# The first layer's rope: both halves copied crosswise by ScalarE, one product with sin on VectorE

## The chip, the core and the metric

The kernel runs on one core of a Trainium2 chip. TensorE (PE in the profile) multiplies matrices into PSUM, VectorE (DVE) and ScalarE (ACT) read PSUM and SBUF and write them, GpSimd (POOL) does small work and some DMAs, and SyncE (SP) issues most DMAs. Each engine works through a queue of its own in order and waits at semaphores for the others. The metric is the device time of one execution in microseconds.

## The reference, cut to what matters

A decoder trunk of two layers on a sequence of 512 positions with a width of 1024, in fp32. The first ("even") layer has 8 heads of retention and, beside them, 8 blocks of a gated linear recurrence (RG-LRU). The second ("odd") layer is differential attention. Both turn q and k by rotary embedding (rope):

```python
def rope(x, pos):
    half = x.shape[-1] // 2
    ...
    x1 = x[..., :half].astype(jnp.float32)
    x2 = x[..., half:].astype(jnp.float32)
    return jnp.concatenate([x1 * cos - x2 * sin, x2 * cos + x1 * sin], axis=-1)

def retention(q, k, v):
    ...
    scores = jnp.einsum('bnihd,bnjhd->bnhij', qc, kc) * decay
    ...

def even_layer(...):
    proj = jnp.einsum('bsd,de->bse', x, w_in)
    q, k, v, g_ret, xb, g_lru = jnp.split(proj, [...], axis=-1)
    q = rope(q.reshape(B, S, RET_HEADS, RET_DK), pos)
    k = rope(k.reshape(B, S, RET_HEADS, RET_DK), pos) * (RET_DK ** -0.5)
    ret = retention(q, k, v.reshape(B, S, RET_HEADS, RET_DV))
```

## The kernel before

**Products.** Every fp32 operand of a product is split into a high and a low half (`split`, L146: a cast to `..h`, by ScalarE as a rule, then on VectorE the difference `..l`, L153), and each product is three matmuls: high by high, low by high, high by low (`mm3`, L155 to L157). Weights come by DMA as raw tiles `w_r` and are split in the same way, so ScalarE and VectorE also carry the weights w0, w1 and on: 1024 columns each.

**The first layer.** Activations lie transposed: a unit (`t_unit`, L196) multiplies one weight tile by x and leaves a tile of 128 channels by 512 positions in one PSUM bank. A list `ev` (L273) sets the order of the units: for heads 0 to 5 in turn the gates gl and gr, the input xb of the recurrence, q and k; v and the output products (out, lo, ro, eo) between them; heads 6 and 7 have another order. The bank pool of the units, `ps_pj`, has four banks, so a unit waits until the tile of four units ago is out of its bank. The scores have two banks (`ps_sc`).

- q and k (L595 to L599): the unit's bank goes through `rope` (L347), which leaves the halves q0h, q0l and so on. L356 multiplies the bank by cos into the tile c; L360 and L361 multiply its lower and upper 64 partitions by sin crosswise into the tile s; L362 adds; `split` follows.
- Retention (`retention`, L479), per head: scores rs from k and q in four blocks (512, 384, 256 and 128 columns), their product with the decay (L487, rsd), the product ro with v, the norm (L498 to L516: squares, a sum by matmul, Ln, Exp, Square, products), then the gate gr (L520) and a split into retm.
- The recurrence (`lru`, L523), per block: ScalarE takes xb from its bank (L526, L528), VectorE adds three taps (L531), xc is split, two products with gate weights (pr, pi), Sigmoid, Tanh, Ln, Exp and Sqrt on ScalarE (L540 to L556, with loads of function tables between them), products on VectorE, a scan (L560), the gate gl (L563).
- Output products: each has its banks summed into y by VectorE (L262, L264).

**Order.** TensorE's and SyncE's queues are written in program order. `Side` (L54) places the matmuls of retention and recurrence between those of the units: a job runs its next piece a set number of ticks later, a tick being one step of three matmuls. VectorE's and ScalarE's queues are put in order by the framework's scheduler, with priorities such as `P_ROPE`.

**The second layer** uses the same `rope` with `swap=True` (L878): ScalarE copies the two halves of the bank crosswise into s (L353, L354), and VectorE multiplies s by sin in one operation (L358) and subtracts (L362). The table `sin` holds the negative in its lower partitions (L950), which is why one form adds and the other subtracts.

Of the kernel before, what the change touches and what calls it, by code (L numbers as in the profile page):

```python
# [11 lines left out]
ALU = mybir.AluOpType  # L12
# [91 lines left out]
def trunk(ctx: ExitStack, tc: tile.TileContext, a):  # L104
    nc = tc.nc
# [22 lines left out]
    def work(name):  # L128
        return wk.tile([P, S], F32, tag="wk", name=name)
# [4 lines left out]
    def bank(pl, tag, name):  # L134
        return pl.tile([P, 512], F32, tag=tag, name=name)

    def pair(pl, shape, tag, name, **kw):
        return tuple(pl.tile(shape, F32R, tag=tag + x, name=name + x, **kw) for x in "hl")
# [4 lines left out]
    def cut(t, *ix):  # L143
        return t[0][ix], t[1][ix]

    def split(src, dst, scale=None, copy=nc.scalar.copy):  # L146
        if scale is not None:
            s = sg[:, scale:scale + 1]
            nc.scalar.activation(out=dst[0], in_=src, func=AF.Identity, scale=s)
            nc.vector.scalar_tensor_tensor(out=dst[1], in0=src, scalar=s, in1=dst[0].bitcast(F32), op0=ALU.mult, op1=ALU.subtract)  # L150
            return
        copy(out=dst[0], in_=src)  # L152
        return nc.vector.tensor_tensor(out=dst[1], in0=src, in1=dst[0].bitcast(F32), op=ALU.subtract)  # L153

    def mm3(out, l, r, start, stop, kinds=range(3), **kw):  # L155
        for n in kinds:
            nc.tensor.matmul(out=out, lhsT=l[n == 2], rhs=r[n == 1], start=start and n == 0, stop=stop and n == 2, **kw)  # L157

    def load(name, shape, src, pl=None, tag=None, bufs=None):
        t = (pl or const).tile(shape, F32, tag=tag or name, name=name, bufs=bufs)  # L160
        nc.sync.dma_start(out=t, in_=src)
        return t
# [27 lines left out]
    def take(ahead):  # L190
        taken[0] += 1
        while len(ready) < min(taken[0] + ahead, len(order)):
            list(fetch())
        return ready[taken[0] - 1]

    def t_unit(act, name):  # L196
        w = take(2)
        ps = bank(ps_pj, "pj", name + "_ps")
        for kt in range(KT):
            mm3(ps, cut(w, ALL, slice(kt * P, kt * P + P)), cut(act, ALL, kt), kt == 0, kt == KT - 1)  # L200
            side.tick()
        return ps
# [78 lines left out]
    for kind, i in ev:  # L281
        if kind in ("ro", "lo", "out"):
            order += [(eo[2 * i + j + n], None) for n in {"ro": (0,), "lo": (8,), "out": (8, 0)}[kind] for j in range(2)]
        else:
            n = 4 if kind == "v" else 1
# [58 lines left out]
    nhalf = const.tile([P, SB], F32, tag="nhalf", name="nhalf")  # L344
    nc.gpsimd.memset(nhalf, -0.5)

    def rope(ps, tag, name, swap=False):  # L347
        with tc.high_priority(P_ROPE):
            s = work(name + "_s")
            h = P // 2  # L350
            if swap:

                nc.scalar.copy(out=s[:h], in_=ps[h:])  # L353
                nc.scalar.copy(out=s[h:], in_=ps[:h])  # L354
            c = work(name + "_c")
            nc.vector.tensor_tensor(out=c, in0=ps, in1=cos, op=ALU.mult)  # L356
            if swap:
                nc.vector.tensor_tensor(out=s, in0=s, in1=sin, op=ALU.mult)  # L358
            else:
                nc.vector.tensor_tensor(out=s[:h], in0=ps[h:], in1=sin[h:], op=ALU.mult)  # L360
                nc.vector.tensor_tensor(out=s[h:], in0=ps[:h], in1=sin[:h], op=ALU.mult)  # L361
            nc.vector.tensor_tensor(out=c, in0=c, in1=s, op=ALU.subtract if swap else ALU.add)  # L362
            r = pair(qkp, [P, S], tag, name)
            split(c, r)
        return r
# [64 lines left out]
    sin = load("sin", [P, S], a["sin"])  # L430
# [152 lines left out]
    for kind, i in ev:  # L583
        if kind == "v":
            if i:
                for j in range(4):
                    side.need(job["ret", j], lambda: j in seen)
            v = v_even(i)
        elif kind == "xb":
            if i % 2 == 0:  # L590
                raw = load(f"gw{i}", [P, 4 * P], a["gw"][i // 2], pl=es, tag="es")
                gw[0] = pair(two, [P, 4 * P], "gw", f"gw{i}", bufs=1)
                split(raw, gw[0])
            job["lru", i] = side.add(lru(i, t_unit(x, f"xb{i}"), mixes(("lru", i // 2))), "lru", 2)
        elif kind == "q":  # L595
            dec[i] = load(f"dec{i}", [P, S], a["dec"][i], pl=two, tag="dec")
            q[i] = rope(t_unit(x, f"q{i}"), "q", f"q{i}")
        elif kind == "k":
            job["ret", i] = side.add(retention(i, q.pop(i), rope(t_unit(x, f"k{i}"), "k", f"k{i}"), v, dec.pop(i), mixes(("ret", i // 2))), "ret", 1, RET_START[i])  # L599
        elif kind in ("ro", "lo", "out"):  # L600
            even_out({"ro": ("ret",), "lo": ("lru",), "out": ("lru", "ret")}[kind], i, f"{kind}{i}")
        else:
            ps = t_unit(x, f"{kind}{i}")
            if len(users) >= 5:
                side.need(job[users[-5]])
            users.append(("ret" if kind == "gr" else "lru", i))
            g = gp.tile([P, S], F32, tag="g", name=f"{kind}{i}")
            silu(ps, g, f"{kind}{i}")
            gates[kind, i] = g
        if (kind, i) == ("gr", 1):  # L610
            for sb in range(SB):
                nc.sync.dma_start(out=y[:, sb], in_=a["x"][sb])
# [4 lines left out]
    h = pair(big, [P, KT, S], "x", "h")  # L617
# [257 lines left out]

    def qk_unit(n, name):
        nonlocal units
        r = rope(t_unit(h, name), n, name, True)  # L878
        if units in later:
            later.pop(units)()  # L880
        units += 1
        return r
# [4 lines left out]
    for kind, i in od:  # L887
# [17 lines left out]
        elif kind == "g":  # L905
            def evac(sb, ps):
                past(i - 1)
                if sb % 2 == 0:
                    pairs[sb] = gp.tile([P, 2, S], F32, tag="g", name=f"og{i}{sb}")
                gates[sb, i] = pairs[sb - sb % 2][:, sb % 2]  # L910
                silu2(ps, gates[sb, i], work(f"og{i}{sb}_t"))

            pairs = {}
            s_unit(h, f"og{i}", False, evac)
            side.need(summed)
            scratch.close()
            qkp = pool("qkp2", 4)
            es = pool("es2", 2)
            mask = load("mask", [P, S], a["mask"], pl=es, bufs=1)
            swap()  # L920
        elif kind == "gv":
            gates_values(i)
        elif kind == "qk":
            om[i] = mix_pair(f"om{i}") if i < 7 else None
            qk = [[qk_unit(n, f"{n}{i}{mp}o") for mp in range(2)] for n in "qk"]
            om[i] = om[i] or cut(pair(big, [P, KT, S], "x", "om7"), ALL, slice(0, 2))
            for qb in range(SB):
                oj[i, qb] = side.add(attention(i, qb, *qk, om[i]), "att", 3, ATT_START[i], ATT_GAP[i])
        else:
            odd_out(i, f"oo{i[0]}", apart=True)  # L930
            if i[0] < 4:
                swap()
# [85 lines left out]
```

## Time and profile before

| what | value |
|---|---|
| median of 3 runs | 919.75 us (919.56 to 919.87) |
| the profiled execution's own time | 920.12 us |
| its span, first to last instruction | 918.4 us |
| granted TensorE clock | 0.997 |
| VectorE, 100 to 150 us: busy | 44.51 of 50 us |
| ScalarE, 50 to 100 us: busy | 37.03 of 50 us |
| DMA from HBM and to it, over the span | 193 GB/s |

The first layer takes about the first 450 us of the span. A row of a timeline has its start, its duration, engine, line, operation, output and inputs, shape, and in brackets the idle time before it with what ended it. Tiles are shown without their buffer numbers, so rq is one name for the squares of all heads; weights keep theirs (w20l). The first matmuls of heads 0, 1, 2 and 7 with their k stand at 66.68, 99.83, 133.24 and 354.03 us.

### The profile page before, as it was taken

To read this page: it belongs to the slowest core of one execution; us is meant where nothing else is said; L and a number is where in the kernel's file an instruction comes from. 1 tells how busy PE (TensorE), PEld (TensorE's weight loads), DVE (VectorE), ACT (ScalarE), POOL (GpSimd) and SP (SyncE) were. 2 spreads that over 40 slices of the span, in tenths; PEclk is the share of its full clock that TensorE was granted. 3 is DMA by queue.
4 is the path that set the end of the run, shared out by engine and by line. 5 is a ranking of instruction groups with operands and counts; after the bars stand their busy time and mean duration, and the time that the engine had idled before them with its cause. 6 is when DMAs were issued, how large, how long until landed. Compare 5 with 4: busy or idle time off the path is not lost.

```text
span 918.4 us, 11868 instructions
## 1 busy us (share of the span) xinstructions
PE 904.9 (99%) x4256; PEld 749.9 (82%) x4256; DVE 717.7 (78%) x1191; ACT 516.3 (56%) x843; POOL 111.6 (12%) x190
## 2 busy tenths in 40 slices
PE   8999999999999999999999999999999999999996
PEld 6888887888888888888888878888888888888885
DVE  5877977958868998897868887748877668877687
ACT  5567787647565668533456666435655355665440
POOL 2310010110102010010101120000120100201112
PEclk9999999999999999999999999999999999999998
DMA  8995463772829371434851226647237382187102
GB/s 279 279 290 149 121 189 92 241 207 58 262 67 287 107 191 64 167 131 149 317 187 70 69 70 228 227 164 252 70 134 248 146 319 93 58 286 249 50 1 91
DMA packets 46522, 152.92 MB, mean 167 GB/s; under 512 B 6144, under 2 KB 6272, under 8 KB 45696
## 3 DMA queue, kind: packets, MB, share of 16 engines
q1 hardware_dynamic: 41472, 135.39, 41.4%
q0 software_dynamic: 4992, 16.78, 9.3%
q8 instruction: 33, 0.54, 0.2%
q14 instruction: 25, 0.20, 0.1%
HBM read 139.57 MB, written 37.75 MB: 193 GB/s over the span
## 4 chain that ended last, share of the span: by engine, by line
PE 85%; DVE 7%; ACT 3%; issue 2%; POOL 1%; DMA 1%; SPq 0%; DVEq 0%; ACTq 0%; POOLq 0%
PE oo_ps L157 7%; PE gr_ps L157 5%; PE out_ps L157 4%; PE q_ps L157 4%; PE gl_ps L157 4%; PE ev_ps L157 4%; PE k_ps L157 4%; PE xb_ps L157 4%; PE po L157 3%; PE as L157 3%; PE ov_ps L157 2%; PE gv3a L157 2%; PE gv2a L157 2%; PE eo_ps L157 2%; PE og_ps L157 2%
## 5 line engine op out<-in xcount | busy, mean ns | idle before, releaser
L670 ACT ACTIVATE e<-as,nm 128x128 f32<-128x128 f32 (+3 forms) x64 | 33.2, 523 | 34.1 <-DVE nm L667 33.9
L677 POOL TENSOR_SCALAR zr<-z 128x1 f32<-128x1 f32 x32 | 16.3, 510 | 248.2 <-ACT e L670 248.2
L709 DVE SCALAR_TENSOR_TENSOR o<-po,ars,og 128x256 f32<-128x256 f32 x32 | 15.5, 484 | 36.8 <-POOL ars L374 36.8
L185 POOL DMA_DIRECT2D t<-t x24 | 18.9, 788 | 158.5 <-DMA t<-in_od_w 152.3
L185 POOL DMA_DIRECT2D t<-in_od_w x24 | 19.0, 793 | 118.6 <-DMA t<-in_od_w 118.6
L706 POOL TENSOR_SCALAR ave<-ss,zr 128x1 f32<-128x1 f32 x32 | 15.8, 493 | 141.7 <-ACT po L703 133.5
L667 DVE CUSTOM_DVE_ANT_0 as<-as,mask 128x128 f32<-128x128 f32 (+3 forms) x64 | 30.5, 507 | 2.3 <-PE as L157 2.3
L703 ACT ACTIVATE po<-po 128x256 f32<-128x256 f32 x32 | 11.9, 371 | 25.5 <-PE po L157 25.3
L548 DVE TENSOR_TENSOR xbp<-xbp,xc 128x512 f32<-128x512 f32 x8 | 5.5, 691 | 17.5 <-ACT xbp L545 17.5
L374 POOL TENSOR_TENSOR ars<-ave,nhalf 128x1 f32<-128x1 f32 x32 | 18.7, 586 | 2.7
L678 DVE SCALAR_TENSOR_TENSOR e<-e,zr,e 128x128 f32<-128x128 f32 (+3 forms) x32 | 17.6, 549 | 0.8
L531 DVE SCALAR_TENSOR_TENSOR xc<-xbp,vecs,xc 128x509 f32<-128x509 f32 (+2 forms) x24 | 17.9, 745 | 0.2
L264 DVE TENSOR_TENSOR y<-oo_ps,y 128x512 f32<-128x512 f32 x24 | 16.0, 684 | 2.2 <-PE oo_ps L157 2.2
L374 POOL TENSOR_TENSOR lrs<-lve,nhalf 128x1 f32<-128x1 f32 x8 | 7.4, 919 | 84.6 <-DVE lve L387 84.6
L487 DVE TENSOR_TENSOR rsd<-rs,dec 128x512 f32<-128x512 f32 (+3 forms) x32 | 15.5, 486 | 2.1 <-PE rs L157 2.1
L540 ACT ACTIVATE t<-pr,vecs 128x512 f32<-128x512 f32 x8 | 5.5, 688 | 17.5 <-PE pr L157 17.5
L682 PE MATMUL wt<-ident,e 128*128 128x128 f32 x80 | 13.9, 272 | 0.0
L152 ACT CAST hh<-ht 128x512 fp32r<-128x512 f32 x8 | 4.7, 587 | 15.7 <-PE ht L627 15.7
L682 PEld LDWEIGHTS wt<-ident,e 128*128 128x128 f32 x80 | 10.5, 140 | 3.4
L556 ACT ACT_TABLE_LOAD x8 | 10.3, 1283 | 4.2 <-DVE xc L555 4.1
L670 ACT ACTIVATION_READ_ACCUMULATOR e<-as,nm 128x1 f32 x64 | 12.5, 195 | 0.0
L675 DVE RECIPROCAL zr<-z 128x1 f32<-128x1 f32 x32 | 5.2, 162 | 9.2 <-ACT e L670 9.1
(2833 smaller groups left out, 3473.2 us busy)
## 6 DMA issues: line engine op xcount, KB each, us to landing
w_r<-in_od_w SPq DMA_DIRECT2D x58, 512.0 KB, 5.8
w_r<-in_ev_w SPq DMA_DIRECT2D x47, 512.0 KB, 4.9
t<-in_od_w SPq DMA_DIRECT2D x48, 256.0 KB, 5.4
sx<-sd SPq DMA_DIRECT2D x24, 512.0 KB, 6.1
w_r<-t SPq DMA_DIRECT2D x24, 512.0 KB, 3.2
w_r<-in_ev_wo SPq DMA_DIRECT2D x16, 512.0 KB, 4.7
w_r<-in_od_wo SPq DMA_DIRECT2D x16, 512.0 KB, 4.6
t<-in_od_w POOLq DMA_DIRECT2D x24, 256.0 KB, 5.5
```

The source lines that it names most:

```text
L157: nc.tensor.matmul(out=out, lhsT=l[n == 2], rhs=r[n == 1], start=start and n == 0, stop=stop and n == 2, **kw)
L185: nc.gpsimd.dma_start(out=dst, in_=two, max_dma_last_dim=4 * D, accum_op=ALU.add)
L264: nc.vector.tensor_tensor(out=yy, in0=ps, in1=yy, op=ALU.add)
L374: nc.gpsimd.tensor_tensor(out=out, in0=var, in1=nhalf[:, :1], op=ALU.pow)
L487: nc.vector.tensor_tensor(out=s[:, :n], in0=ps[:, :n], in1=dec[:, :n], op=ALU.mult)
L531: nc.vector.scalar_tensor_tensor(out=xc[:, sh:], in0=xb[:, :S - sh], scalar=conv_w(w, c), in1=xc[:, sh:], op0=ALU.mult, op1=ALU.add)
L667: nc.vector.tensor_tensor_reduce(out=ps[:, :n], in0=ps[:, :n], in1=mask[:, S - n:], scale=-QK_SCALE, scalar=3.0e38, op0=ALU.add, op1=ALU.m ...
L670: nc.scalar.activation(out=e, in_=ps[:, :n], func=AF.Exp, scale=-1.0, bias=nm, accum_out=z[:, mp:mp + 1])
L677: nc.gpsimd.tensor_scalar(out=zr[:, 1:2], in0=z[:, 0:1], scalar1=z[:, 0:1], scalar2=EPS, op0=ALU.mult, op1=ALU.mult)
L678: nc.vector.scalar_tensor_tensor(out=ee[0], in0=ee[1], scalar=zr[:, 0:1], in1=ee[0], op0=ALU.mult, op1=ALU.add)
L682: nc.tensor.transpose(out=pt[:, kb * P:kb * P + P], in_=ee[0][:, kb * P:kb * P + P], identity=ident)
L706: nc.gpsimd.tensor_scalar(out=ve, in0=ss, scalar1=zr[:, 1:2], scalar2=None, op0=ALU.add)
```

## The change

`rope` loses its argument `swap`: every call now takes the form with two ScalarE copies of 64 partitions, one product with sin over 128 partitions, and a subtraction. It concerns the 16 ropes of the first layer (8 heads, q and k). The 16 of the second layer stay as they are.

```diff
-    def rope(ps, tag, name, swap=False):
+    def rope(ps, tag, name):
         with tc.high_priority(P_ROPE):
             s = work(name + "_s")
             h = P // 2
-            if swap:
-                nc.scalar.copy(out=s[:h], in_=ps[h:])
-                nc.scalar.copy(out=s[h:], in_=ps[:h])
+            nc.scalar.copy(out=s[:h], in_=ps[h:])
+            nc.scalar.copy(out=s[h:], in_=ps[:h])
             c = work(name + "_c")
             nc.vector.tensor_tensor(out=c, in0=ps, in1=cos, op=ALU.mult)
-            if swap:
-                nc.vector.tensor_tensor(out=s, in0=s, in1=sin, op=ALU.mult)
-            else:
-                nc.vector.tensor_tensor(out=s[:h], in0=ps[h:], in1=sin[h:], op=ALU.mult)
-                nc.vector.tensor_tensor(out=s[h:], in0=ps[:h], in1=sin[:h], op=ALU.mult)
-            nc.vector.tensor_tensor(out=c, in0=c, in1=s, op=ALU.subtract if swap else ALU.add)
+            nc.vector.tensor_tensor(out=s, in0=s, in1=sin, op=ALU.mult)
+            nc.vector.tensor_tensor(out=c, in0=c, in1=s, op=ALU.subtract)
...
-        r = rope(t_unit(h, name), n, name, True)
+        r = rope(t_unit(h, name), n, name)
```

The order of instructions on TensorE, GpSimd and SyncE is the same before and after. On ScalarE 32 copies join and on VectorE 16 products go, and the scheduler puts these two queues in another order in the first layer. The lines behind `rope` have numbers lower by 5 in the changed kernel.

ScalarE's queue in head 1, from the Ln of the recurrence's block 1 (r1) on, before (ro0 and rq0 are head 0's retention and its squares):

```order
L552 ACTIVATE r1_847<-t1_835 128x512
L553 ACT_TABLE_LOAD
L553 ACTIVATE r1_847<-r1_847 128x512
L498 ACTIVATE rq0_876<-ro0_863 128x512
L152 CAST rq0h_878<-rq0_876 128x512
L152 CAST q1h_888<-q1_c_883 128x512
L556 ACT_TABLE_LOAD
L556 ACTIVATE r1_847<-t1_835 128x512
L509 ACT_TABLE_LOAD
L509 ACTIVATE rq0_876<-rv0_925,epsb_119 128x512
```

The same piece of ScalarE's queue now:

```order
L547 ACTIVATE r1_849<-t1_837 128x512
L352 COPY q1_s_884<-q1_ps_804 64x512
L493 ACTIVATE rq0_878<-ro0_865 128x512
L353 COPY q1_s_884<-q1_ps_804 64x512
L152 CAST rq0h_880<-rq0_878 128x512
L548 ACT_TABLE_LOAD
L548 ACTIVATE r1_849<-r1_849 128x512
L152 CAST q1h_891<-q1_c_887 128x512
L551 ACT_TABLE_LOAD
L551 ACTIVATE r1_849<-t1_837 128x512
L352 COPY k1_s_942<-k1_ps_903 64x512
L353 COPY k1_s_942<-k1_ps_903 64x512
```

The Exp of r1 (L553, now L548) has moved behind q1's copies, the square and the cast of rq0, and k1's two copies stand between the Sqrt (L556, now L551) and the norm's Ln.

VectorE's queue ahead of xc2l, the low half of the recurrence's block 2, for which TensorE's pr2 waits, before:

```order
L153 TENSOR_TENSOR w19l_1107<-w19_r_1105,w19h_1106 128x1024
L531 SCALAR_TENSOR_TENSOR xc2_1062<-xbp2_1060,vecs_203,xc2_1062 128x509
L153 TENSOR_TENSOR r11l_1054<-rsd11_1051,r11h_1053 128x384
L531 SCALAR_TENSOR_TENSOR xc2_1062<-xbp2_1060,vecs_203,xc2_1062 128x510
L487 TENSOR_TENSOR rsd12_1084<-rs12_1080,dec1_792 128x256
L531 SCALAR_TENSOR_TENSOR xc2_1062<-xbp2_1060,vecs_203,xc2_1062 128x511
L457 TENSOR_TENSOR gr2_1099<-gr2_ps_1043,gr2_sg_1100 128x512
L487 TENSOR_TENSOR rsd13_1121<-rs13_1117,dec1_792 128x128
L153 TENSOR_TENSOR r12l_1087<-rsd12_1084,r12h_1086 128x256
L153 TENSOR_TENSOR w20l_1185<-w20_r_1183,w20h_1184 128x1024
L153 TENSOR_TENSOR r13l_1124<-rsd13_1121,r13h_1123 128x128
L153 TENSOR_TENSOR xc2l_1068<-xc2_1062,xc2h_1067 128x512
```

The same piece now:

```order
L526 SCALAR_TENSOR_TENSOR xc2_1066<-xbp2_1064,vecs_203,xc2_1066 128x509
L153 TENSOR_TENSOR w19l_1111<-w19_r_1109,w19h_1110 128x1024
L526 SCALAR_TENSOR_TENSOR xc2_1066<-xbp2_1064,vecs_203,xc2_1066 128x510
L482 TENSOR_TENSOR rsd13_1125<-rs13_1121,dec1_794 128x128
L526 SCALAR_TENSOR_TENSOR xc2_1066<-xbp2_1064,vecs_203,xc2_1066 128x511
L153 TENSOR_TENSOR r13l_1128<-rsd13_1125,r13h_1127 128x128
L153 TENSOR_TENSOR r12l_1091<-rsd12_1088,r12h_1090 128x256
L452 TENSOR_TENSOR gr2_1103<-gr2_ps_1047,gr2_sg_1104 128x512
L153 TENSOR_TENSOR w20l_1190<-w20_r_1188,w20h_1189 128x1024
L153 TENSOR_TENSOR xc2l_1072<-xc2_1066,xc2h_1071 128x512
```

rsd13 has moved ahead of the last tap of xc2 (128x511), and r13l and r12l ahead of gr2; w20l stands just ahead of xc2l in both.

VectorE's queue in head 6, from k6's rope to the sums of the product lo into y, before:

```order
L362 TENSOR_TENSOR k6_c_2821<-k6_c_2821,k6_s_2820 128x512
L153 TENSOR_TENSOR r53l_2852<-rsd53_2849,r53h_2851 128x128
L554 SCALAR_TENSOR_TENSOR xc6_2694<-t6_2773,r6_2785 128x512
L153 TENSOR_TENSOR k6l_2827<-k6_c_2821,k6h_2826 128x512
L555 SCALAR_TENSOR_TENSOR xc6_2694<-xc6_2694,r6_2785 128x512
L153 TENSOR_TENSOR r52l_2808<-rsd52_2805,r52h_2807 128x256
L264 TENSOR_TENSOR y_202<-lo2_ps00_2840,y_202 128x512
L264 TENSOR_TENSOR y_202<-lo2_ps01_2841,y_202 128x512
L264 TENSOR_TENSOR y_202<-lo2_ps10_2866,y_202 128x512
```

The same piece now, from the product with cos on:

```order
L355 TENSOR_TENSOR k6_c_2836<-k6_ps_2765,cos_212 128x512
L153 TENSOR_TENSOR r53l_2866<-rsd53_2863,r53h_2865 128x128
L356 TENSOR_TENSOR k6_s_2833<-k6_s_2833,sin_214 128x512
L264 TENSOR_TENSOR y_202<-lo2_ps00_2854,y_202 128x512
L357 TENSOR_TENSOR k6_c_2836<-k6_c_2836,k6_s_2833 128x512
L552 SCALAR_TENSOR_TENSOR t6_2786<-t6_2786,xc6_2706 128x512
L553 SCALAR_TENSOR_TENSOR r6_2798<-r6_2798,xc6_2706 128x512
L153 TENSOR_TENSOR k6l_2841<-k6_c_2836,k6h_2840 128x512
L554 TENSOR_TENSOR r6_2798<-r6_2798,xbp6_2704 128x512
L264 TENSOR_TENSOR y_202<-lo2_ps01_2855,y_202 128x512
L555 SCALAR_TENSOR_TENSOR xc6_2706<-t6_2786,r6_2798 128x512
L264 TENSOR_TENSOR y_202<-lo2_ps10_2880,y_202 128x512
```

The two gate operations on xc6 (L554 and L555, now L549 and L550) and r52l have moved ahead of k6's rope, and the three sums into y, which stood together, now stand one by one between the rope's and the recurrence's operations.

## The prediction

> **What bounds the kernel now.** I read the page's busy line first, then who waited for whom with TensorE as the waiting engine, then TensorE's timeline at those waits.
>
> ```profile
> PE 904.9 (99%) x4256; PEld 749.9 (82%) x4256; DVE 717.7 (78%) x1191; ACT 516.3 (56%) x843; POOL 111.6 (12%) x190
> ```
> TensorE has no room: only work that holds it up can move the end. The wait view up to 450 us, which holds the first layer, names four such waits after the start-up:
>
> ```profile
> PE out_ps L157 <- ACT xc L528: 0.5, 1, 0.5
> PE pr L157 <- DVE xc7l L153: 0.4, 1, 0.4
> PE out_ps L157 <- DVE gl L457: 0.3, 1, 0.3
> PE rs L157 <- DVE rsd L487: 0.2, 1, 0.2
> ```
> A matmul row (0.39 us) outlasts the 0.23 us between two starts, so the true delay is read from the starts:
>
> ```profile
> 114.17 0.39 PE L157 MATMUL pr<-xc2h,gw2h 128*128 128x512 f32 x1
> 114.53 0.50 PE L157 MATMUL pr<-xc2l,gw2h 128*128 128x512 f32 x1
> ...
> 139.08 0.40 PE L157 MATMUL out_ps<-w22h,lrum0l 128*128 128x512 f32 x1
> 139.83 0.50 PE L157 MATMUL out_ps<-w21h,lrum0h 128*128 128x512 f32 x1 [0.35 <-DVE gl L457]
> ...
> 140.40 0.40 PE L157 MATMUL out_ps<-w21h,lrum0l 128*128 128x512 f32 x1
> 141.03 0.38 PE L157 MATMUL rs<-q2h,k2h 128*128 128x256 f32 x1 [0.24 <-DVE rsd L487]
> ...
> 141.95 0.40 PE L157 MATMUL out_ps<-w22h,lrum0l 128*128 128x512 f32 x1
> 142.84 0.51 PE L157 MATMUL out_ps<-w21h,lrum0h 128*128 128x512 f32 x1 [0.50 <-ACT xc L528]
> ...
> 342.61 0.39 PE L157 MATMUL pr<-xc7h,gw6h 128*128 128x512 f32 x1
> 343.39 0.50 PE L157 MATMUL pr<-xc7l,gw6h 128*128 128x512 f32 x1 [0.40 <-DVE xc7l L153]
> ```
> Less 0.23 for each pair, and with the 0.1 by which the second matmul after a wait comes late: 0.25 at pr2, 1.9 between 139 and 143, 0.67 at pr7, some 0.2 at pr3 near 149, read the same way. **About 3.0 us is all that a faster first layer can win**; everything else there is TensorE at full pitch. All four waits are for VectorE and ScalarE, so these two stretches count:
>
> ```profile
> 83.00:100.00 17.00, 17.00 (x80) 14.22 (x79) 14.49 (x22) 15.18 (x19) 0.78 (x1) 1.00 0.12 17
> ...
> 100.00:115.00 15.00, 15.00 (x69) 12.18 (x69) 15.00 (x25) 10.04 (x16) 1.56 (x2) 1.00 0.65 188
> 116.00:143.00 27.00, 25.91 (x117) 20.68 (x116) 21.89 (x33) 23.77 (x30) 3.93 (x5) 1.00 0.56 156
> ```
> (columns: TensorE, weight loads, VectorE, ScalarE). ScalarE is the fuller of the two in 83-100 (15.18 of 17) and in 116-143 (23.77 of 27); between them VectorE has no pause at all (15.00 of 15).
>
> **What an edit costs.** Removed and added per rope:
>
> ```profile
> L360 DVE TENSOR_TENSOR q_s<-q_ps,sin x8: 693/693/693, 53.3 to 338.2; 64x512 f32<-64x512 f32 x8
> L361 DVE TENSOR_TENSOR q_s<-q_ps,sin x8: 683/684/685, 54.0 to 338.9; 64x512 f32<-64x512 f32 x8
> ...
> L358 DVE TENSOR_TENSOR q00o_s<-q00o_s,sin x1: 681/681/681, 462.1 to 462.1; 128x512 f32<-128x512 f32 x1
> L353 ACT COPY q00o_s<-q00o_ps x1: 585/585/585, 460.3 to 460.3; 64x512 f32<-64x512 f32 x1
> ```
> A half costs VectorE as much as a whole tile, so a rope saves 0.69 there, 11 us in 16 ropes, and ScalarE gets two copies of 0.585, 19 us in all. Matmuls and DMAs keep their order; only ScalarE's and VectorE's orders change. Neither total is on the path; what is new there is a wait, shown by the second layer, which already does it so:
>
> ```profile
> 460.29 0.58 ACT L353 COPY q00o_s<-q00o_ps 64x512 f32<-64x512 f32 x1
> 460.88 0.58 ACT L354 COPY q00o_s<-q00o_ps 64x512 f32<-64x512 f32 x1
> ...
> 461.50 0.69 DVE L356 TENSOR_TENSOR q00o_c<-q00o_ps,cos 128x512 f32<-128x512 f32 x1
> ```
> The product with cos, which reads the same PSUM bank, starts only after the second copy ends (461.46). So VectorE's queue now stands still whenever ScalarE comes late to the copies. Before, L356 needed TensorE alone.
>
> **Step 1, head 1 (83 to 116).** The chain is walked through the new rows of the order, each with its duration and spacing from these rows of before.
>
> ```profile
> 86.56 0.63 ACT L553 ACTIVATE r<-r 128x512 f32<-128x512 f32 x1
> 90.49 0.63 ACT L556 ACTIVATE r<-t 128x512 f32<-128x512 f32 x1
> 95.15 0.63 ACT L511 ACTIVATE rq<-rsd 128x512 f32<-128x512 f32 x1
> ...
> 98.80 0.69 DVE L153 TENSOR_TENSOR k1l<-k_c,k1h 128x512 fp32r<-128x512 f32 x1
> 110.66 0.74 DVE L531 SCALAR_TENSOR_TENSOR xc<-xbp,vecs,xc 128x511 f32<-128x511 f32 x1
> 113.79 0.69 DVE L153 TENSOR_TENSOR xc2l<-xc,xc2h 128x512 fp32r<-128x512 f32 x1
> ...
> 99.83 0.40 PE L157 MATMUL rs<-q1h,k1h 128*128 128x512 f32 x1
> 106.59 0.28 PE L157 MATMUL rs<-q1h,k1h 128*128 128x256 f32 x1
> ```
> The Exp of r (86.56) gets q1's copies, the square and rq0h ahead of it: 88.82. VectorE's gate update waits for it, rope's difference stands behind that, q1h behind the difference; so the Sqrt (90.49) starts at 92.72. k1's copies stand behind it: the square of rsd (95.15) starts at 98.41. k1h and the rest of k1l follow: k1l starts at 99.66 (0.86 late) and ends at 100.35, just when its matmul (third of the scores at 99.83) wants it. From there VectorE's saturated stretch begins late and holds more: lrum0l (0.6) and rsd13 (0.2), which stood outside it, and 0.5 of waits for lrum0h. The last tap of xc2 (110.66) starts at 112.86. On the way the first product with dec of head 1 ends at 107.28 where the matmul at 106.59 wants its bank: TensorE loses 0.7. Then r13l, r12l, gr2 and w20l stand ahead of xc2l as before: 115.81 to 116.50, so pr2's second matmul starts at 116.52, not 114.53: **+2.0 us**, the 0.7 included. Nothing hides it, since the xc2l of before was already 0.25 late. Lower bound +0.6 (only k1l's lateness arrives, less the 0.25), upper +2.6.
>
> **Step 2, head 2 and out0 (116 to 149).** ScalarE is nearly full here, and four copies (2.3) join while w23's cast (1.06) moves behind; the Sqrt stands earlier. Set from pr2's end, the evacuation of xb3 (L526, L528), for which TensorE waits at 142.84, stands behind retm0h, which waits for L520; walked through, it ends as long after pr2 as before, within 0.1. With pr2 2.2 later on ScalarE it ends at 145.0: TensorE resumes 2.2 late. k2l, now behind the scan, makes the scores wait 1.1 at 135, and the waits at 139.08 and 140.40 go, but both lie under the last one. xc3l then needs no wait at 149 (-0.2). After step 2 the sum stands at **+2.0**. Bounds +0 (those 2 us of waits swallow step 1) and +3.
>
> **Heads 0 and 3 to 5: 0.** The same walk ends k0l at 67.03 where its matmul starts at 67.15; in heads 3 to 5 k's low half is ready over 2 us early. Without that cover a rope's chain is 0.4 longer each time (two copies 1.17, less one 0.69).
>
> **Step 3, heads 6 and 7 (300 to 357).**
>
> ```profile
> 315.11 0.39 PE L157 MATMUL lo_ps<-w49h,lrum2h 128*128 128x512 f32 x1
> 319.75 0.39 PE L157 MATMUL lo_ps<-w49h,lrum2h 128*128 128x512 f32 x1
> 321.11 0.39 PE L157 MATMUL lo_ps<-w49h,lrum2h 128*128 128x512 f32 x1
> ...
> 316.13 1.88 DVE L264 TENSOR_TENSOR y<-lo_ps,y 128x512 f32<-128x512 f32 x3
> ...
> 354.50 0.40 PE L157 MATMUL rs<-q7h,k7l 128*128 128x512 f32 x1
> 351.22 0.60 ACT L152 CAST k7h<-k_c 128x512 fp32r<-128x512 f32 x1
> ```
> k6's copies run behind the Exp of r6 (to 314.3); the product with cos gives k6's bank back at 315.46, where lo wants it at 315.11: +0.4. The three sums into y no longer stand together (316.13) but between rope and gate rows: the second ends at 320.65, the third at 322.4. lo21 (319.75, now 320.14) and lo30 (321.11) wait for them: +1.3 together. At 343 the wait for xc7l goes, since it now stands ahead of rope's difference and without two products: -0.67. But k7's copies, w58h and two activations stand ahead of k7h: 353.6 instead of 351.22, and k7l ends at 354.95, each 1.3 later with the shift. Its matmul (354.50) starts at 356.26: **+1.8** for step 3. Bounds -0.7 (only the xc7l wait goes) and +2.5.
>
> **Sum.** +2.0 and +1.8: 3.8 us. The profiled execution took 920.12 us (span 918.4, 1.7 around it); the runs' median, 919.75, is 0.4 lower, so 919.75 + 3.8 = 923.5 us.
>
> **Rivals.** *VectorE's saving decides (faster).* VectorE is full in 100-115, and all four waits lead through it; with 0.69 less per rope it could come early. If k1l is ready before 100.3 and xc2l before 114.2, all 3.0 us go: 916.7 us. Against it: the rope is fed by ScalarE, which in 83-100 has 1.8 us of pause for 2.3 us of copies. The deciding point is that k1l. [...]
>
> *Swallowed (no change).* TensorE's old waits at 139-143 take up step 1, and step 3 ends near the -0.67 and +1.3 of its first half: +0 to +1.8, some 921 us. For it: the ends of step 1 hang on a few tenths at 100.35 and 107.28. Against: the evacuation of xb3 follows pr2.
>
> *More of it (slower still).* Ropes hold the bank and the work tiles longer; if each of the remaining heads too loses 0.4 us, 2 us come on top: 925.5.
>
> **Chances.** Forecast 0.59, swallowed 0.24, faster 0.12, more 0.05. 0.2% is 1.8 us, about what a measurement of this kernel can tell from no change: slower by more 0.64, within 0.25, faster by more 0.11. The range is the sum of the bounds of steps 2 (which holds step 1) and 3 on 919.75: 0 and -0.7 give 919.0, 3 and 2.5 give 925.3; it leaves out the faster case and the one of more, 0.17.
>
> **What would show it.** Right: L356's idle time names L353/L354's copies in heads 0 to 7; k1l ends near 100.4; pr2's second matmul starts near 116.5; out_ps resumes near 145; lo's matmuls wait for L264; head 7's scores wait for k7. Wrong: pr2 at 114 to 115 (step 1 falls), TensorE resuming before 143 (the faster rival), or no wait between 315 and 322 (step 3).

## The result, and the profile after

| | before | after |
|---|---|---|
| median | 920.15 us (919.56 to 920.66, 6 runs) | 926.81 us (925.84 to 927.38, 6 runs) |
| ratio | | 1.0072 [1.0062, 1.0082] |
| span of the profiled execution | 918.4 us | 925.2 us |

The change makes the kernel 6.7 us slower. The page of the changed kernel, busy times of the engines:

```profile
PE 907.7 (98%) x4256; PEld 749.7 (81%) x4256; DVE 707.1 (76%) x1175; ACT 535.5 (58%) x875; POOL 112.1 (12%) x190
```

VectorE is 10.6 us shorter and ScalarE 19.2 longer, as counted. TensorE does the same matmuls and waits more. Who waits for whom with TensorE as the waiting engine, 20 to 450 us, changed kernel (total, times, longest):

```profile
PE pr L157 <- DVE xc2l L153: 1.1, 1, 1.1
PE rs L157 <- ACT k7h L152: 1.0, 1, 1.0
PE out_ps L157 <- ACT xc L523: 0.7, 1, 0.7
PE rs L157 <- DVE k2l L153: 0.7, 1, 0.7
PE pi L157 <- DVE rsd L482: 0.6, 1, 0.6
PE rs L157 <- ACT k2h L152: 0.5, 1, 0.5
PE rs L157 <- DVE rsd L482: 0.4, 1, 0.4
PE rs L157 <- DVE k0l L153: 0.2, 1, 0.2
PE lo_ps L157 <- DVE y L264: 0.2, 1, 0.2
```

Two of the four old waits are gone (for the gate gl, and xc7l); k's halves, which nobody waited for, now make up four lines. A wait hides the end of the matmul ahead of it (a row lasts 0.39 us, two starts stand 0.23 apart), so I compared the starts of the same matmul in both traces. TensorE's timeline of the changed kernel, at the places where its distance to before grows:

```profile
67.92 0.50 PE L157 MATMUL rs<-q0h,k0l 128*128 128x512 f32 x1 [0.20 <-DVE k0l L153]
...
100.86 0.50 PE L157 MATMUL rs<-q1h,k1h 128*128 128x512 f32 x1
...
101.67 0.50 PE L157 MATMUL rs<-q1h,k1l 128*128 128x512 f32 x1
...
108.60 0.38 PE L157 MATMUL rs<-q1h,k1h 128*128 128x256 f32 x1 [0.39 <-DVE rsd L482]
...
117.79 0.50 PE L157 MATMUL pr<-xc2l,gw2h 128*128 128x512 f32 x1 [1.11 <-DVE xc2l L153]
...
137.19 0.50 PE L157 MATMUL rs<-q2h,k2h 128*128 128x512 f32 x1 [0.51 <-ACT k2h L152]
...
138.64 0.50 PE L157 MATMUL rs<-q2h,k2l 128*128 128x512 f32 x1 [0.71 <-DVE k2l L153]
...
146.97 0.50 PE L157 MATMUL out_ps<-w21h,lrum0h 128*128 128x512 f32 x1 [0.72 <-ACT xc L523]
...
310.86 0.50 PE L157 MATMUL pi<-xc6h,gw6h 128*128 128x512 f32 x1 [0.60 <-DVE rsd L482]
...
360.20 0.50 PE L157 MATMUL rs<-q7h,k7h 128*128 128x512 f32 x1 [1.03 <-ACT k7h L152]
...
360.93 0.50 PE L157 MATMUL rs<-q7h,k7l 128*128 128x512 f32 x1
```

Added lateness by stretch, each the start here less the start before, less what was late already:

| stretch | forecast | measured |
|---|---|---|
| start-up to 12 us (not the change) | none | +0.38 |
| head 0, third matmul of the scores | 0 | +0.39 |
| head 1, up to pr2's second matmul | +2.0 | +2.48 (0.25, 0.35, 0.63, 1.25) |
| head 2 and out0, net after 153 us | 0 | +0.71 |
| heads 3 to 5 | 0 | within 0.1 |
| heads 6 and 7 | +1.8 | +2.47 (pi6 0.78, lo 0.77, pr7 -0.42, scores of head 7 1.34) |
| second layer | none | +0.3 |

A wait also makes the next matmul 0.1 late (behind k2h's wait the starts are 137.19 and 137.53, 0.34 apart instead of 0.23); in this table and below, that 0.1 stands with the next place. With its own 0.1, head 0 costs 0.47, head 1 2.38, and heads 6 and 7 cost 2.55 (pi6 0.87, lo 0.80, pr7 -0.66, scores of head 7 1.54). The start-up differs by -0.6 to +0.5 us between the traces of all runs, which are alike up to there, and the second layer by up to 1.6 (head1), so neither row is the change's.

The windows of the changed kernel (TensorE, weight loads, VectorE, ScalarE) show who got emptier:

```profile
83.00:100.00 17.00, 17.00 (x79) 14.19 (x79) 10.63 (x16) 15.32 (x20) 0.78 (x1) 1.00 0.19 44
100.00:115.00 15.00, 14.53 (x65) 11.19 (x64) 14.32 (x24) 12.01 (x19) 0.78 (x1) 1.00 0.39 118
116.00:143.00 27.00, 24.67 (x110) 19.59 (x110) 19.49 (x28) 24.14 (x32) 3.16 (x4) 1.00 0.59 161
```

In 83-100 VectorE falls from 14.49 to 10.63 us: far more than two ropes save, so work has moved out of this stretch. The timelines of ScalarE and VectorE there show why:

```profile
85.50 0.63 ACT L547 ACTIVATE r<-t 128x512 f32<-128x512 f32 x1
86.15 0.58 ACT L352 COPY q_s<-q_ps 64x512 f32<-64x512 f32 x1
86.76 0.60 ACT L493 ACTIVATE rq<-ro 128x512 f32<-128x512 f32 x1
87.38 0.58 ACT L353 COPY q_s<-q_ps 64x512 f32<-64x512 f32 x1
...
89.92 0.63 ACT L548 ACTIVATE r<-r 128x512 f32<-128x512 f32 x1
91.91 0.62 ACT L152 CAST q1h<-q_c 128x512 fp32r<-128x512 f32 x1 [1.36 <-DVE q_c L357]
```
```profile
87.99 0.69 DVE L355 TENSOR_TENSOR q_c<-q_ps,cos 128x512 f32<-128x512 f32 x1 [3.08 <-ACT q_s L353]
88.64 0.69 DVE L153 TENSOR_TENSOR rq0l<-rq,rq0h 128x512 fp32r<-128x512 f32 x1
89.25 0.69 DVE L356 TENSOR_TENSOR q_s<-q_s,sin 128x512 f32<-128x512 f32 x1
```

VectorE stands 3.08 us for ScalarE's second copy, which stands behind an Ln and a square; then ScalarE stands 1.36 us for VectorE's difference. The two in-order queues hold each other up in turn. VectorE's waits for a second copy, 20 to 450 us:

```profile
DVE q_c L355 <- ACT q_s L353: 8.6, 3, 3.1
DVE k_c L355 <- ACT k_s L353: 3.1, 1, 3.1
```

So VectorE stands still for a copy in four of the sixteen ropes only (q0, q1, q4 and k7), and q4's wait costs TensorE nothing. In the other twelve, other work fills VectorE's queue until the copies are done. In all 48 ropes of this trace the product with cos begins behind the end of the second copy out of the same bank, by 0.03 to 1.08 us (at q1 the copy ends at 87.96 and the product starts at 87.99).

### The profile page after: what moved, and what is told of

The parts are those of the page before. It is cut to its first block, busy times and chain, and to the rows that moved or that the text cites. A ratio compares the mean times of both kernels' runs of the same rounds, so it can differ in the third digit from the quotient of the medians.

```text
span 925.2 us, 11892 instructions
## 1 busy us (share of the span) xinstructions
PE 907.7 (98%) x4256; PEld 749.7 (81%) x4256; DVE 707.1 (76%) x1175; ACT 535.5 (58%) x875; POOL 112.1 (12%) x190
## 4 chain that ended last, share of the span: by engine, by line
PE 76%; ACT 9%; DVE 9%; issue 3%; DMA 2%; POOL 1%; SPq 0%; DVEq 0%; ACTq 0%; POOLq 0%
PE oo_ps L157 6%; PE out_ps L157 4%; PE ev_ps L157 4%; PE q_ps L157 4%; PE gr_ps L157 4%; PE xb_ps L157 3%; PE gl_ps L157 3%; PE po L157 3%; PE as L157 2%; PE ov_ps L157 2%; PE gv3a L157 2%; PE eo_ps L157 2%; PE og_ps L157 2%; PE k_ps L157 2%; PE gv3b L157 2%
## 5 line engine op out<-in xcount | busy, mean ns | idle before, releaser
L549 DVE SCALAR_TENSOR_TENSOR xc<-t,r 128x512 f32<-128x512 f32 x8 | 5.5, 692 | 11.0 <-ACT r L548 11.0
L677 PEld LDWEIGHTS wt<-ident,e 128*128 128x128 f32 x80 | 10.5, 140 | 3.4
L708 PEld LDWEIGHTS po<-ident,o 128*128 128x128 f32 x64 | 8.9, 140 | 4.2
```

Of the source, the lines that this page charges most:

```text
L677: nc.tensor.transpose(out=pt[:, kb * P:kb * P + P], in_=ee[0][:, kb * P:kb * P + P], identity=ident)
```

## The experiments

Theory A, from the first reading: TensorE is late where k or xc has no cover, because a link of rope now runs through ScalarE. Rivals: B, ScalarE's added time costs the same wherever it stands; C, the loss is an accident of the scheduler's new order. D came later: what counts is what stands behind the copies in ScalarE's queue.

All medians are of 4 to 11 executions, against the kernel before in the same series (919.98 to 920.26).

| run | median us | against before | ratio, 95% interval |
|---|---|---|---|
| heads012 | 924.26 | +4.1 | [1.0033, 1.0058] |
| heads345 | 920.31 | +0.2 | [0.9993, 1.0010] |
| heads67 | 922.84 | +2.7 | [1.0018, 1.0041] |
| head1 | 922.88 | +2.9 | [1.0019, 1.0042] |
| heads02 | 921.61 | +1.4 | [1.0007, 1.0025] |
| konly | 922.79 | +2.7 | [1.0017, 1.0039] |
| qonly | 923.23 | +3.1 | [1.0019, 1.0044] |
| occupancy | 928.84 | +8.7 | [1.0079, 1.0110] |
| occupancy_behind | 927.92 | +7.8 | [1.0068, 1.0096] |
| vector_saving | 920.16 | +0.2 | [0.9994, 1.0012] |
| cos_first | 923.52 | +3.4 | [1.0024, 1.0049] |
| before_vector_cast | 918.73 | -1.25 | [0.9979, 0.9996] |
| change_vector_cast | 929.25 | +9.3 | [1.0082, 1.0110] |
| cos_first_vector_cast | 925.41 | +5.15 | [1.0050, 1.0077] |
| before_low_priority | 921.90 | +1.7 | [1.0008, 1.0026] |
| change_low_priority | 929.41 | +9.2 | [1.0087, 1.0114] |

### Which heads

The kernel before, with the copies only where a name is listed (here for heads 6 and 7; the others alike):

```diff
-            s = work(name + "_s")
+            s, swap = work(name + "_s"), swap or name in ("q6", "k6", "q7", "k7")
```

heads012: 

> Copies only in heads 0 to 2 (6 of 16 ropes); heads 3 to 7 as before. Theory A (the loss is made where k or the convolution's low half is only just in time, so that TensorE waits for a chain that now runs through the copies): +3.6 us over the kernel before, with TensorE late by about 0.4 at 67, 0.6 at 100, 0.6 at 107, 1.2 at 115 and 4 at 150 us, and nothing after that. Theory B (ScalarE's added work costs the same wherever it stands): 6 of 16 parts of the 6.7 us, +2.5 us, spread evenly. Theory C (a new order in the two queues shifts waits at random): no prediction by head; the sites of the full change would not come back.

heads345: 

> Copies only in heads 3 to 5. Theory A: k's low half is 1.4 to 3.7 us early there even in the changed kernel, so 0 (within 0.3 us). Theory B: +2.5 us. Theory C: anything between -1 and +2.5.

heads67: 

> Copies only in heads 6 and 7. Theory A: the stretch from 300 to 357 us as in the full change: +0.8 where pi6's bank waits for rsd51, +0.8 at lo's two matmuls, -0.4 at pr7, +1.3 at head 7's scores: +2.5 us in all. Theory B: 4 of 16 parts, +1.7 us. Theory C: not these sites.

Measured +4.1, +0.2 and +2.7: together 7.0, where the whole change is 6.7. TensorE's sites are those of the full change to 0.1 us (in heads67: pi6 +0.75, lo +0.77, pr7 -0.42, head 7's scores +1.33). Theory A holds by place, B falls: six ropes of heads 3 to 5 cost nothing that can be measured. C in its plain form falls too, since the sites come back one by one.

head1: 

> Copies only in head 1 (q1 and k1). In the run with heads 0 to 2, TensorE lost 0.4 by 70 us, 2.5 at 100 to 115 us, and 0.9 net from 133 to 150 us. If step 1 of the prediction holds (q1's copies push the Exp, k1's stand behind the Sqrt, k1l and the convolution's xc2l come late): xc2l's matmul late by 2.0 to 2.5 us here too, about as much as there without head 0's 0.4. If step 2 holds (the shift persists through the old waits at 139 to 143, since the evacuation of the recurrence's input follows): +2.0 to +2.5 us over the kernel before at the end. If the old waits swallow it: +0.3 to +1. If head 0's lateness was needed for it: xc2l late by less than 1.

TensorE's timeline of head1, pr2's second matmul:

```profile
116.62 0.50 PE L157 MATMUL pr<-xc2l,gw2h 128*128 128x512 f32 x1 [1.09 <-DVE xc2l L153]
```

It stands 2.1 us behind its place before, 2.4 if one counts from the 0.30 by which this execution was ahead at 12 us. After 143 us it is 2.8 by the same count, 0.4 of it from lrum0's gate at 139.83: the old waits there swallow nothing. So step 1 and its persistence hold with head 0 untouched.

heads02: 

> Copies only in heads 0 and 2. Head 1 alone gave 2.5 us by the sites up to 150 us, heads 0 to 2 together 3.7. If each head has its own price: +1.2 us (k0l 0.4 late at 67, k2l late at 133). If the waits at 139 to 143 us swallow head 2's own lateness unless head 1 has used them up: head 0's 0.4 alone arrives, +0 to +0.6, and k2l's wait shows at 133 to 135 but is given back by 143.

k2's scores are late by 1.24 and 0.98 at 133 us. The profiled execution also shows TensorE at half its clock for 3.4 us here (0.51 from 137.30 to 140.75, last section), which adds 1.6; 2.1 of the whole is given back between 139 and 150. The median, +1.4, in which most executions lack the half clock, less head 0's 0.47 leaves some 0.9 for head 2, not far from the 0.71 of the full change. So the old waits swallow a part of head 2's lateness, without head 1 as with it, and the number for swallowing it whole (+0 to +0.6) was wrong. With head1's +2.9 the +1.4 adds up to the 4.1 of heads012 within the intervals.

konly and qonly, the same edit by q and k:

konly: 

> Copies only in the 8 ropes of k. Theory A1 (k's own chain to its low half is longer, and the scores wait for it): nearly the whole loss, +4 to +6 us, at 67, 100, 133 and 354 us. Theory A2 (the walk of the prediction: q1's copies push the Exp of the recurrence back, and everything of head 1 behind it): about half, +2.5 to +4 us; k1's low half is late by about 0.6 instead of 0.9 and xc2l by 1 instead of 2.5. Theory B (ScalarE's time alone counts, wherever it stands): 8 of 16 parts, +3.3 us.

qonly: 

> Copies only in the 8 ropes of q. Theory A1: 0 to +1 us, since q's low half is early everywhere. Theory A2: +2 to +3.5 us, with k1l and xc2l late through the Exp of r1. Theory B: +3.3 us. This run and the one with k alone need not add up to the whole: where both are just in time, the waits share their cover.

+2.7 and +3.1. With k alone, head 1 loses nothing and k2l's 0.78 is given back by 141; what remains is lo (1.0) and head 7 (1.5). With q alone, the norm's rq1 comes 0.9 late at 123, lrum0's gate 1.5 at 139 and pi6's bank 0.76. In neither is xc2l late. Head 1's 2.5 us need both q1's and k1's copies, as the walk of step 1 had it (q1's ahead of the Exp, k1's behind the Sqrt); A1, with k's own chain alone, falls. Both medians lie in A2's ranges by luck: A2 named xc2l as late in both, and the loss stands elsewhere.

### ScalarE's time, VectorE's time

occupancy adds two copies per rope to the kernel before that feed nothing; occupancy_behind puts the same two lines behind the split:

```diff
             nc.vector.tensor_tensor(out=c, in0=c, in1=s, op=ALU.subtract if swap else ALU.add)
+            if not swap:
+                nc.scalar.copy(out=s[:h], in_=c[h:])
+                nc.scalar.copy(out=s[h:], in_=c[:h])
```

occupancy: 

> The kernel before, with two further ScalarE copies of 64x512 in each of the 16 ropes of the first layer, which read the finished sum of the rope and write a tile that nothing reads any more (the result is unchanged, VectorE keeps its three products). ScalarE's busy time rises as in the change (+19 us), but no link of rope runs through ScalarE. Theory A: most of the loss is gone; what stands behind the copies in ScalarE's own queue is late by 0.6 to 1.2 at the places where ScalarE has no pause (90 to 100 and 116 to 143 us): +0.5 to +2 us, and no wait of L356. Theory B: +6.7 us, as in the change, or more, since VectorE saves nothing. Theory C: unknown, between -1 and +3.

occupancy_behind: 

> As the run named occupancy (the kernel before with two idle copies per rope of the first layer, result unchanged), but with the copies written behind the split, so that they stand behind the casts of q's and k's high halves in ScalarE's queue and not ahead of them. There the scores of head 1 waited 1.5 us for k1h, whose cast stood behind the copies. If what counts is what stands behind the copies in ScalarE's queue (theory D): head 1's scores late by 0 to 0.5 instead of 1.8, pi6's wait and the one for the gate lrum0 near 140 us mostly as there, in all +3 to +6 us. If ScalarE's added time counts wherever it stands (theory B): +8.7 us again. If only a link of rope through ScalarE counts (theory A): 0 to +1 us.

Measured +8.7 and +7.8. Theory A's number is far off: ScalarE's time costs more than the change does, though nothing waits for these copies. TensorE's longest waits in occupancy:

```profile
PE out_ps L157 <- DVE gl L460: 1.8, 1, 1.8
PE pi L157 <- DVE rsd L490: 1.7, 1, 1.7
PE rs L157 <- ACT k1h L152: 1.5, 1, 1.5
```

These are again places without cover: what stands behind the copies on ScalarE (k1h's cast here, whose copies of 0.62 each stand right ahead of it) is late by their time and by what was late ahead of them. That is theory D, and for occupancy_behind it was right by place (head 1's scores 0.6 late instead of 2.0) but not in size: TensorE waited 1.9 us for the norm's rq1 at 123 us instead, and lrum0's gate came later still. In occupancy's trace some 1.2 us of the loss are, by estimate, the half clock of the last section (0.51 from 146.2 to 149.6); its one execution with a mean clock of 0.997 still took 928.73 us. In occupancy_behind every execution has some of it, judged by the mean clock (0.992 to 0.994, in the kernel before 0.997 or 0.998; in the trace about 10 us at half clock, estimated from the windows of the last section), so its 7.8 is not the price of the copies alone.

vector_saving is VectorE's half of the change:

```diff
-                nc.vector.tensor_tensor(out=s[:h], in0=ps[h:], in1=sin[h:], op=ALU.mult)
-                nc.vector.tensor_tensor(out=s[h:], in0=ps[:h], in1=sin[:h], op=ALU.mult)
+                nc.vector.tensor_tensor(out=s, in0=ps, in1=sin, op=ALU.mult)
```

> VectorE's side of the change alone: in the first layer's ropes one product with sin over 128 partitions in place of the two over 64, read straight from the bank, and no ScalarE copies. The halves are not exchanged, so the rotation is not computed; the instructions are otherwise those of the kernel before. VectorE is 0.69 us shorter per rope, 11 us in all. If VectorE's saving is worth what the faster rival said: -2 to -3.0 us. If it is worth only what lies on the path (the waits for the gate lrum0 at 139 us and for xc7l at 343 us): -0.5 to -1.5. If nothing: within 0.3.

Nothing, +0.2. The saving itself arrives: k1l starts at 96.48 where it started at 98.80. But nobody waited for it. TensorE's waits in this run, 20 to 450 us:

```profile
PE rs L157 <- DVE rsd L487: 1.2, 2, 0.8
PE out_ps L157 <- ACT xc L528: 0.8, 1, 0.8
```

The wait for xc7l is gone (-0.66 at 343 us), but 0.63 comes back at head 7's rsd; -0.52 at 139 us comes back within 4 us as waits for rsd and for ScalarE's evacuation. Here the measurement decides against the faster rival: VectorE was full in a stretch (15.00 of 15 us in 100 to 115 before, 14.14 here), yet shortening it was worth nothing, and ScalarE's time was dear (occupancy, +8.7).

### The place of the product with cos, and of the cast

cos_first is the change with two lines moved (first layer only):

```diff
+            nc.vector.tensor_tensor(out=c, in0=ps, in1=cos, op=ALU.mult)
             nc.scalar.copy(out=s[:h], in_=ps[h:])
             nc.scalar.copy(out=s[h:], in_=ps[:h])
-            nc.vector.tensor_tensor(out=c, in0=ps, in1=cos, op=ALU.mult)
```

> The changed kernel with the first layer's product with cos written ahead of the two copies, so that VectorE's product waits for TensorE alone and ScalarE's copies wait for VectorE (they share the bank). If VectorE's queue standing behind ScalarE's copies is what costs (theory A, head of line): 2 to 5 of the 6.7 us come back, +2 to +4.5 over the kernel before. If the length of the chain over two engines costs (copies, product with sin, difference, split, one after the other in either order): about as much as the full change, +6 to +8, and ScalarE's copies then show the waits for L354 and L361's product that VectorE showed for them.

+3.4: half of the loss is gone, with the same instructions on each engine. VectorE's timeline, the same q1 as above:

```profile
84.81 0.68 DVE L354 TENSOR_TENSOR q_c<-q_ps,cos 128x512 f32<-128x512 f32 x1
87.97 0.69 DVE L359 TENSOR_TENSOR q_s<-q_s,sin 128x512 f32<-128x512 f32 x1 [2.48 <-ACT q_s L356]
```

The product starts 3.2 us earlier and the rest of the rope then needs one operation less behind the copies. Against the full change, TensorE is 1.27 us less late at xc2l, 1.7 at k2 and 1.2 at k7h; head 0's k0l comes later still (+1.15, in the change +0.39), and new waits come for xc3 (1.3) and rq5l (1.25).

The cast to q's and k's high half on VectorE, without the change, with it, and with both edits:

```diff
-            split(c, r)
+            split(c, r, copy=nc.scalar.copy if swap else nc.vector.tensor_copy)
```

before_vector_cast: 

> The kernel before with the same cast on VectorE and no copies: ScalarE 0.6 us shorter per rope, VectorE as much longer, one hop less. Theory D: head 1 to 2's scores and the Exp behind q1's cast come earlier; the four old waits are mostly for VectorE, which gets more: -1 to +1.5 us. The difference to the run with the change and this cast is what the copies cost where the hop is gone: +1 to +3 us by theory D, 6.7 us if the copies cost the same whatever stands around them (theory B).

change_vector_cast: 

> The changed kernel with the cast to the high half of q and k (first layer) on VectorE instead of ScalarE. ScalarE then gets two copies and loses one cast per rope (+0.58 net instead of +1.17), and one hop between the engines goes (in the changed kernel ScalarE stands 1.36 us idle for q1's difference, ahead of the cast). Theory D (ScalarE's queue in the full stretches, with what stands behind the copies and the cast): at least half of the loss comes back, +1 to +3.5 us over the kernel before. If VectorE's own load is the next limit (its time per rope goes back to four or more operations): +5 or more, with VectorE full in 100 to 115 us.

cos_first_vector_cast: 

> The changed kernel with both edits: the product with cos ahead of the copies, and the cast of q and k (first layer) on VectorE. The change with the first alone is +3.4, with the second alone +9.3 us over the kernel before; the kernel before with the cast is -1.25. If VectorE's wait behind ScalarE's copies is what makes the fuller VectorE costly: the two edits add up, +3.4 less 1.25, i.e. +1 to +3 us. If the copies with a fuller VectorE cost as such, in either order: +7 to +10. If it is the order that the scheduler happens to give: anything between.

-1.25, +9.3 and +5.15. **before_vector_cast beats both kernels.** It moves work the other way: 6 us more on VectorE (717.7 to 723.8 in the busy line), 9 us less on ScalarE, one hop between them less; of the waits from 20 to 450 us one is left in the list:

```profile
PE out_ps L157 <- ACT xc L528: 0.4, 1, 0.4
```

Theory D's number for change_vector_cast (+1 to +3.5) was plainly wrong, and so were both numbers for what the copies cost where the hop is gone: from -1.25 to +9.3 it is 10.5 us, where D said 1 to 3 and B 6.7. Three of its four executions have a mean clock of 0.995 or 0.996 and took 929.21 to 930.05 us; the fourth, at 0.997, took 927.89, so up to 1.4 of the 9.3 may be the half clock of the last section. That fourth one is the profiled one. Its trace puts 2.5 us at a sum into y and 1.5 at w24l, both late on VectorE:

```profile
PE lo_ps L157 <- DVE y L264: 2.5, 1, 2.5
PE out_ps L157 <- DVE w24l L153: 1.5, 1, 1.5
```

The order with cos first takes back 4.1 us here (2.7 less that half clock), as it took back 3.3 without the cast; but the cast still costs 1.8 us beside the copies, where it wins 1.25 alone. Why it does so was not settled: the sums into y stand elsewhere in VectorE's queue in each of these kernels, and no run held that order fixed.

### The order by priority

```diff
-P_ROPE, P_SCORES, P_SQUARE, P_GROUP, P_VALUE = 50, 13, 60, 5, 60
+P_ROPE, P_SCORES, P_SQUARE, P_GROUP, P_VALUE = 20, 13, 60, 5, 60
```

before_low_priority: 

> The kernel before with rope's priority 20 instead of 50, the control for the next run. Rope's operations stand later behind the recurrence's: between -1 and +2 us, by the order alone.

change_low_priority: 

> The changed kernel with rope's priority 20 instead of 50: in head 1 the Exp of r1 and its Sqrt stand ahead of q1's second copy and of k1's copies, so the recurrence is not held up there, and q1 and k1 come later instead. If the copies' place ahead of the Exp is what cost (step 1 of the prediction): xc2l's matmul about 1 to 1.5 us earlier than in the change, k1's scores as late or later; +3 to +5.5 over the kernel before in all. If the copies cost the same wherever they stand: +6 to +8. A pure accident of order: could be 0.

+1.7 and +9.2, so the change costs 7.5 us in this order and 6.7 in the other: no accident of one order. The 9.2 lies above every number expected for it. A part is half clock: judged by the mean clock (0.994 to 0.996) no execution is free of it, and in the trace the clock is 0.52 from 69.7 to 73.1 and 0.83 over 140 to 150 us, by estimate 1.6 and 1.7 us of TensorE's time. The copies' place matters all the same: with the Exp ahead of them, xc2l adds 0.76 instead of 1.25 and head 1 about 1.2 instead of 2.4, but TensorE now waits 1.7 us for k0h in head 0. The priority holds for the second layer's ropes too; nothing shifts there (before_low_priority's lateness is 1.75 us at 400 and 1.81 at the end).

## Why the prediction was right and where it was not

It said 923.5 (919.0 to 925.3); 926.8 was measured. The sign and nearly all places were right, and the mechanism (a wait for ScalarE's copies in VectorE's queue) is there at q0, q1 and k7; the size was short by 3 us, 6.7 for 3.8. What failed are the terms put at zero for heads 0 and 2, and in step 3 pi6's wait, which was missed, and the scores of head 7, which were mis-sized. By the table the steps lack 0.39 (head 0), 0.48 (step 1), 0.71 (head 2) and 0.67 (step 3), and the start-up and second layer of this trace bring 0.7. The median of the kernel before, 920.15 with the change and 919.75 in the sum, makes 0.4 of the distance in time.

- **Bounds.** That TensorE alone sets the end and that only some 3.0 us can be won was not contradicted: VectorE's whole saving won nothing, the best kernel 1.25 us.
- **What an edit costs.** The counts and durations held. L355's idle time names the copies in four ropes (3.08 us at q1), not in heads 0 to 7 as was said.
- **Heads 0 and 3 to 5: 0.** For heads 3 to 5 right. For head 0 this step failed: it set k0l's end at 67.03 for a matmul at 67.15, 0.12 us of margin, and gave it no bound. k0l ended at 67.87, or 67.49 without the start-up, and the matmul came 0.39 later. VectorE's timeline ahead of it shows the kind of hop that was not in the walk:

```profile
64.12 0.68 DVE L357 TENSOR_TENSOR k_c<-k_c,k_s 128x512 f32<-128x512 f32 x1
64.72 0.68 DVE L553 SCALAR_TENSOR_TENSOR r<-r,xc 128x512 f32<-128x512 f32 x1
65.44 0.69 DVE L554 TENSOR_TENSOR r<-r,xbp 128x512 f32<-128x512 f32 x1
66.05 1.22 DVE L153 TENSOR_TENSOR w14l<-w_r,w14h 128x1024 fp32r<-128x1024 f32 x1
67.19 0.68 DVE L153 TENSOR_TENSOR k0l<-k_c,k0h 128x512 fp32r<-128x512 f32 x1
```

  Operations on different tiles start 0.60 apart, but the product that needs the result right ahead of it comes 0.72 behind (64.72 to 65.44); before, k0l stood between these two. On ScalarE the copy at 86.15 above starts 0.65 behind the Ln, 0.02 after its end. A few hops of 0.1 eat a margin of 0.12; that they make up the whole 0.46 is not shown. The "0.4 longer each time" is 0.48 by its own numbers (1.17 less 0.69).
- **Step 1.** Right in each of its links. Against its own numbers the Exp came at 89.92 instead of 88.82, the Sqrt at 93.85 instead of 92.72, xc2l at 117.06 instead of 115.81: 1.1 to 1.25 late throughout, of which 0.8 stood ahead of head 1. The step itself added 2.48 (2.38 without head 0's 0.1; head1 alone: 2.4) where 2.0 was said, within its bounds of 0.6 to 2.6.
- **Step 2.** The persistence held (head1 keeps its 2.4 us and gains 0.4). What failed is the term for head 2: k2's waits were put wholly under the one for xb3's evacuation. They measured 1.67 us (1.1 was said), the waits at 139 and 141 gave back 0.93, and 0.7 arrived, because the evacuation slips too: it ended at 146.92, not 145.0.
- **Step 3.** +1.8 said, +2.47 measured, near the upper bound, by errors of both signs. Missed: pi6's wait for rsd51, whose score bank comes free late behind q6's rope (0.78; qonly shows it, konly doesn't). Too large: lo (0.77, not 1.7; k6's bank, 0.4 of it, held up nothing). Too small: the scores of head 7 (1.34 added, against 0.73 in the sum). The relief at pr7, said as -0.67, is -0.66.
- **The faster rival** asked whether k1l is ready in time; the copies make it late, and without them (vector_saving) its 2.3 us come to nothing. Its error was to take saturation for a place on the path.
- **The swallowing rival** is a real mechanism: it takes up a part of head 2's lateness, with head 1's copies and without (heads02), and nothing of step 1.
- **More of it** was nearest in time (925.5), by luck: it priced heads 3 to 5 too, which cost nothing. Heads 0 and 2 did lose 0.39 and 0.71, where k's halves came late.
- **The range** ended below the result since head 0 stood in it at zero and head 2 at 0.4 at most (3.0 less step 1's 2.6): the upper bounds of steps 2 and 3 were 3.0 and 2.5, where 3.58 (heads 0 to 2) and 2.47 came. Besides, start-up and second layer (0.7 together in that trace) had no place in it.

What stays open: how the 6.7 us divide between ScalarE's time as such and VectorE's wait behind it. The order with cos first takes away half, in two settings; idle copies alone cost as much as the whole change and more, when VectorE keeps its products. The two need not add, since they may use up the same cover. Nor did any run hold the scheduler's order fixed: every edit here also reorders VectorE's and ScalarE's queues.

## What to carry to other kernels

An engine that is full for a while is worth unloading only if the waits of the bounding engine end on it because of its amount of work (in vector_saving 12.0 us less on VectorE, 705.7 for 717.7, left the time at +0.2 us); try the saving alone (even in a kernel that leaves out a step, as vector_saving leaves out the exchange) before paying for it elsewhere. A step moved to another in-order engine takes on that engine's queue (3.08 us of standing still at q1): write what needs only the old producer ahead of what waits for the new one. Price a chain by its hops and give each margin below two or three hops (here 0.1 us each) a bound of its own.

## What the hardware showed beside

**Behind waits close together four traces show TensorE at half its clock, for some 3.4 us or more.** In heads02, windows of TensorE around k2's two waits (granted clock is the third number from the end):

```profile
134.00:137.30 3.30, 1.50 (x6) 0.94 (x6) 3.27 (x5) 3.27 (x5) 0.00 (x0) 1.00 0.00 0
137.30:140.75 3.45, 3.45 (x9) 2.64 (x9) 3.42 (x6) 3.24 (x5) 0.00 (x0) 0.51 0.03 7
140.75:144.00 3.25, 3.25 (x16) 2.75 (x15) 3.25 (x6) 1.89 (x4) 0.00 (x0) 0.99 0.16 23
```

In the first 3.30 us, which hold the waits for k2h (1.08) and k2l (0.71), TensorE was busy for 1.50; in the 3.45 us behind them the granted clock is 0.51. Matmuls start 0.43 apart there instead of 0.23: eight such spacings lose 1.6 us on top of the waits. The same shows in change_low_priority from 69.7 to 73.1 us (1.17 busy of 3.30, then 0.52) and between 140 and 150 us (0.83 over these 10 us), in occupancy from 146.2 to 149.6 us (1.77 busy of 4.20, then 0.51) and in occupancy_behind, where 120 to 130, 140 to 150 and 150 to 160 us have 0.83, 0.83 and 0.82. The changed kernel's waits at 137 to 139 us leave TensorE busy for 2.78 of the 4.00 us from 136 to 140 and cost no clock (1.00). It does not come every time: of the eleven executions of heads02, the three with a mean clock of 0.995 took 922.6 to 923.2 us, the eight with 0.997 or 0.998 took 920.6 to 921.9. So in the profiled execution the waits' price was more than their length, and, judged by the mean clock, it was not in most others of the same kernel. What decides it is not shown, and TensorE's idle time does not settle it alone: heads02's two waits are 1.79 us together, while change_vector_cast's wait of 2.5 us for the sum into y lies between 300 and 330 us, where the clock is 1.00.
